# A two-layer diffusion backbone: the output projection of layer 1, three weight tiles split earlier, its first sums begun early, and x loaded into other places

## The chip, the cores and the metric

The kernel runs on one core of one Trainium2 chip. Five engines work side by side, each in its own fixed order: TensorE (PE: matmuls; PEld: loading of their stationary operand), VectorE (DVE), ScalarE (ACT), GpSimd (POOL) and SyncE (SP), which issues nearly all DMAs. They wait for each other by semaphores. The metric is the device time of one execution in microseconds (us).

## The reference, cut to what matters

Input: x (512 tokens of 1024), a context of 256 tokens, conditioning vectors, and float32 weights of two layers. Each layer is a mixer (attention) followed by a SwiGLU feed-forward network (FFN, hidden size 2816), both behind an RMS norm with adaptive scale and shift, both added to x through a gate. Layer 0 has windowed and dense attention; layer 1 has differential attention with 8 heads. Layer 1 is what the change touches:

```python
def finish(o):                                   # o: (b, n, 8 heads, 128)
    o = _rms(o, subln_w) * (1.0 - lam_init)      # norm over each head's 128
    return o.reshape(o.shape[0], o.shape[1], -1) @ w_out
o_x = _diff_attend(q_x, concat(k_c, k_x), concat(v_c, v_x), lam)
out_x = finish(o_x)                              # (512 x 1024) @ (1024 x 1024)
...
x = x + gx1 * ax                                 # the way out of the mixer
x = x + gx2 * _swiglu(_rms(x, norm_ffn_w[l]) * (1.0 + scx2) + shx2, ffn_w_in[l], ffn_w_out[l])
```

In the last layer only the 512 tokens of x go on; the context serves as keys and values.

## The kernel before, in words

**Tiles.** Tokens lie in tiles of 128: t = 0 to 3 are x, 4 and 5 the context. The model width 1024 is 8 K-tiles of 128. The operand of a projection lies transposed in hT (columns of x) and hTc (columns of the context), each as a pair: a rounded part "hi" and the rest "lo", both in float32r. A weight tile is split likewise: `unit` (L318) loads it into one of two raw buffers (tag "raw", L90), ACT rounds it (L326, woh), and DVE or POOL subtracts (L327, wol). Each product is then three matmuls, hi·hi, hi·lo, lo·hi (in the way out: L747, L748, L749). A tile of wor, woh and wol is one K-tile of the output weights, 512 KB raw.

**Layer 1's attention.** `in_proj1` (L593) makes q, k and v of one head for one token tile: projection (L422 to L424), copy qkv (L630), rotation, normalisation with rs_q on POOL (L156, L157), operands qd and kd, transposes (L651, L657). `attend1` (L664) has two parts: scores sc (L673, L674), maximum mx (DVE L676), exponentials e (ACT L678) and their combination (DVE L685); then transposes ppt (L692), the product with v, av (L700), and the norm of the head's result: o (ACT L702, L705), rs_o (POOL), o again (DVE L707). `Staggered` (L873) runs the second part of one tile behind the first part of the next. The stage's loop (L1063 on) goes over heads h and token tiles t, and `emit` (L1054) puts in the projections for a head about one head ahead: after h = 6, t = 0 the context tiles and tiles 0 and 1 of head 7 are in, after t = 2 all.

**The way out (OutProj, L718).** When all head projections are emitted (h = 7, t = 0), their pools are closed, and `out_units` (L710) loads and splits the 8 K-tiles of the output weights into the place that came free; every third raw tile goes to a place of its own, wor. `operand` (L725) loads the tile's x (`load_x`, L330), transposes its result o in two halves of 4 K-tiles (L737), and splits each half into hT (ACT L738, DVE L739). `sums` (L741) makes two halves of 512 columns, each 8 K-tiles of 3 matmuls in one PSUM bank; for tiles 0 to 2 both halves use the bank acc0, at low priority. `residual` (L426) multiplies by the gate (L429, into rtmp, one buffer) and adds to x (L430), on POOL for tiles 0 to 2 and on DVE for tile 3. Then `norm_steps` (L282) prepares FFN's operand: square (ACT L291), rs_n (POOL), scaling (ACT L293), transposes npt (PE L298), scale and shift (L304, L306), split (L308, L309). Its two work tiles, the room, are here the places of the context's hTc, two sets, used in turn.

**Places.** The tag "xo" has six places of 128 x 1024: layer 1's four results o_t lie in four of them, and x of tiles 0 and 1 can be loaded into the other two; x of tiles 2 and 3 takes the places of o of tiles 0 and 1 after their transposes. Split weights of the way out and of FFN share eight places each (tags whi and wlo).

**Order.** The order of each engine's instructions is fixed before the run: a planner goes by the order of the program, by priorities (`tc.high_priority`) and by its own estimate of the times.

Of the kernel before, what the change touches and what calls it, by code (L numbers as in the profile page):

```python
# [10 lines left out]
F32 = mybir.dt.float32  # L11
F32R = mybir.dt.float32r
# [51 lines left out]
def backbone(es: ExitStack, tc: tile.TileContext, x, c, ctx, c_ctx, mod_w, mod_b, norm_mix_w, norm_ffn_w,  # L64
# [48 lines left out]
    def f32(ap):  # L113
        return ap.bitcast(F32)
# [203 lines left out]
    def unit(pool, views, shape, bufs, name, sub=None, new_tile=raw_tile):  # L318

        raw = new_tile(shape, name + "r")  # L320
        for dst, src in views(raw):
            turn["load"] = nc.sync.dma_start(dst, src)
        p_hi, p_lo = pool if isinstance(pool, tuple) else (pool, pool)
        hi = p_hi.tile(shape, F32R, name=name + "h", tag="whi", bufs=bufs)
        lo = p_lo.tile(shape, F32R, name=name + "l", tag="wlo", bufs=bufs)
        nc.scalar.copy(hi, raw)  # L326
        (sub or nc.vector).tensor_sub(lo, raw, f32(hi))  # L327
        return hi, lo
# [378 lines left out]
        nc.vector.scalar_tensor_tensor(oc, oc, r, subln, ALU.mult, ALU.mult)  # L707


    def out_units(wp, w_out, subs=(nc.gpsimd,), rooms=(raw_tile,)):  # L710
        ws = []
        for k in range(KT):
            def views(raw, k=k):
                yield raw, w_out[0, k * P:(k + 1) * P, :]
            ws.append(unit(wp, views, [P, D], 8, "wo", subs[k % len(subs)], rooms[k % len(rooms)]))
        return ws

    class OutProj:  # L718

        def __init__(self, l, ws, o_t, xs, pool):  # L720
            self.l, self.ws, self.o_t, self.xs, self.g = l, ws, o_t, xs, {}
            for i in range(2 if l == 0 else 1):
                self.g[i] = gate_row(l, 2, i, pool)

        def operand(self, t):  # L725
            if self.xs[t] is None:
                self.xs[t] = load_x(t, self.l == 1)
            ohi, olo = tile_T(0, t), tile_T(1, t)
            if self.l == 0:
                nc.scalar.copy(ohi, self.o_t[t])  # L730
                nc.gpsimd.tensor_sub(olo, self.o_t[t], f32(ohi))
                return
            for q in range(2):
                pt = tr_tile("opt", [P, 4, P])
                for k in range(4):
                    kk = 4 * q + k
                    nc.tensor.transpose(pt[:, k, :], self.o_t[t][:, kk * P:(kk + 1) * P], ident)  # L737
                nc.scalar.copy(ohi[:, 4 * q:4 * q + 4], pt)  # L738
                nc.vector.tensor_sub(olo[:, 4 * q:4 * q + 4], pt, f32(ohi[:, 4 * q:4 * q + 4]))  # L739

        def sums(self, t, bank=None, pool=None, add=nc.vector):  # L741
            ohi, olo = tile_T(0, t), tile_T(1, t)
            for n in range(2):
                ps = acc_tile("ops", one=bank)
                for k in range(KT):
                    a, b = (z[:, n * 512:(n + 1) * 512] for z in self.ws[k])
                    nc.tensor.matmul(ps, ohi[:, k, :], a, start=k == 0, stop=False)  # L747
                    nc.tensor.matmul(ps, ohi[:, k, :], b, start=False, stop=False)  # L748
                    nc.tensor.matmul(ps, olo[:, k, :], a, start=False, stop=k == KT - 1)  # L749
# [194 lines left out]
    for b in range(4):  # L944
# [9 lines left out]
        if b == 3:  # L954
            att.flush()
            wp.close()
            even.close()
            wp = Pool("w0", "right")
            opa = Pool("opa")
            xs = [None] * NT  # L960
            oproj = OutProj(0, out_units(wp.pool, ev_w_out), o_t, xs, opa.pool)
        for t in order:
            for hp in range(2):
                if hp == 1:
# [191 lines left out]
```

## Time and profile before

| | us |
|---|---|
| median of 3 runs | 1808.97 (1807.68 to 1810.03) |
| profiled execution, its own time | 1809.96 |
| its span in the trace | 1808.2 |
| PE busy in the span | 1738.5 (96%) |
| layer 1's heads, first to last combination of exponentials (L685) | 1078.4 to 1362.1 |
| matmuls of layer 1's way out | 1354.5 to 1420.7 |

All times inside the execution count from the start of the span. A row of the order of time gives start, duration, engine, line, operation, output <- inputs, shapes and count; a bracket at its end tells how long the engine idled before it, and what released it. A busy PE is not PE at its peak: the granted clock (PEclk) says which share of full speed it had.

### The profile page before, as it was taken

The page shows a single profiled execution, that of the slowest core. Times are in us where ns is not written, and L with a number is a line of the kernel's source. Part 1 is how long each engine was busy: PE and PEld are TensorE (multiplying, and loading weights), DVE is VectorE, ACT ScalarE, POOL GpSimd, SP SyncE. Part 2 cuts the span into 40 slices and gives each one's busy share as a digit, 9 for nine tenths or more (in the row PEclk, how much of TensorE's full clock was granted, in tenths as well). Part 3 has the DMA queues.
Part 4 walks back from the last instruction along what each step waited for, and adds up shares of the span by engine and source line. Part 5 has one row for each costly group of instructions (what it writes and reads, how often), then busy time and mean ns, then how long its engine had stood idle before and what let it go on. Part 6 is the DMA issues. An engine that isn't in the chain of part 4 may idle for free. (4 is left out here: it accounts for less than half of the span.)

```text
span 1808.2 us, 26146 instructions
## 1 busy us (share of the span) xinstructions
PE 1738.5 (96%) x9958; PEld 1455.4 (80%) x9958; DVE 999.7 (55%) x1703; ACT 823.0 (46%) x1726; POOL 649.6 (36%) x840
## 2 busy tenths in 40 slices
PE   6999999999999999999999989999998999999998
PEld 4887776678888888888888889999986878888886
DVE  4765554444265555554543556766684455655653
ACT  6555555545354444343332656666573521231220
POOL 2774554632163344232220486667643200000000
PEclk8999999999999999999999999999999999999999
DMA  9112322303543234334320311111102333232331
GB/s 315 43 50 71 105 94 75 112 24 112 178 154 105 94 105 142 115 117 139 118 85 2 102 53 59 36 43 47 34 36 94 105 95 91 83 123 76 89 98 47
DMA packets 152477, 165.64 MB, mean 92 GB/s; under 512 B 16480, under 2 KB 139936, under 8 KB 152352
## 3 DMA queue, kind: packets, MB, share of 16 engines
q1 hardware_dynamic: 152000, 163.77, 28.9%
q8 instruction: 78, 1.28, 0.3%
q14 instruction: 47, 0.39, 0.1%
q10 hardware_dynamic: 352, 0.21, 0.0%
HBM read 159.73 MB, written 4.22 MB: 91 GB/s over the span
## 5 line engine op out<-in xcount | busy, mean ns | idle before, releaser
L785 PE MATMUL pg<-hT,wgh 128*128 128x512 f32 (+1 forms) x736 | 242.7, 384 | 0.0
L785 PE MATMUL pu<-hT,wuh 128*128 128x512 f32 (+1 forms) x736 | 242.2, 383 | 0.0
L429 DVE TENSOR_TENSOR dps<-dps,g 128x512 f32<-128x512 f32 x200 | 135.8, 697 | 142.4 <-PE dps L839 137.1
L837 PE MATMUL dps<-wdh,hdh 128*128 128x512 f32 x440 | 177.3, 404 | 8.7 <-ACT hdh L435 5.2
L838 PE MATMUL dps<-wdl,hdh 128*128 128x512 f32 x440 | 175.1, 398 | 0.0
L839 PE MATMUL dps<-wdh,hdl 128*128 128x512 f32 x440 | 166.4, 396 | 0.0
L785 PEld LDWEIGHTS pg<-hT,wgh 128*128 128x128 f32 x736 | 136.4, 188 | 30.9 <-issue 1.2
L785 PEld LDWEIGHTS pu<-hT,wuh 128*128 128x128 f32 x736 | 135.7, 188 | 28.7
L785 PE MATMUL pg<-hT,wgl 128*128 128x512 f32 (+1 forms) x368 | 141.4, 384 | 0.0
L785 PE MATMUL pu<-hT,wul 128*128 128x512 f32 (+1 forms) x368 | 140.9, 383 | 0.0
L430 DVE TENSOR_TENSOR x<-x,dps 128x512 f32<-128x512 f32 x200 | 133.2, 683 | 3.3
L422 PE MATMUL inps<-wih,hT 128*128 128x384 f32 x384 | 133.6, 348 | 0.9 <-ACT qkv L470 0.5
L424 PE MATMUL inps<-wih,hT 128*128 128x384 f32 x384 | 130.9, 342 | 0.0
L423 PE MATMUL inps<-wil,hT 128*128 128x384 f32 x384 | 130.7, 340 | 0.0
L206 ACT ACTIVATE modw<-modw,cols 128x256 f32<-128x256 f32 x192 | 82.0, 498 | 71.5 <-DMA modw<-in_mod_w_dram 64.5
L837 PEld LDWEIGHTS dps<-wdh,hdh 128*128 128x128 f32 x440 | 83.1, 189 | 31.7 <-ACT hdh L435 5.8
L327 DVE TENSOR_TENSOR wul<-wur,wuh 128x1024 fp32r<-128x1024 f32 x44 | 53.9, 1225 | 83.1 <-ACT wuh L326 83.1
L839 PEld LDWEIGHTS dps<-wdh,hdl 128*128 128x128 f32 x440 | 82.6, 188 | 19.9
L812 DVE TENSOR_TENSOR pu<-sg,pu 128x768 f32<-128x768 f32 (+1 forms) x44 | 36.4, 828 | 111.3 <-PE pu L785 96.9
L785 PE MATMUL pu<-hTc,wuh 128*128 128x256 f32 x352 | 97.9, 282 | 0.0
L838 PEld LDWEIGHTS dps<-wdl,hdh 128*128 128x128 f32 x440 | 83.3, 189 | 18.2 <-issue 0.4
L785 PE MATMUL pg<-hTc,wgh 128*128 128x256 f32 x352 | 97.8, 282 | 0.0
(235 smaller groups left out, 4289.4 us busy)
## 6 DMA issues: line engine op xcount, KB each, us to landing
modw<-in_mod_w_dram SPq DMA_DIRECT2D x96, 512.0 KB, 3.9
wgr<-in_ffn_w_in_dram SPq DMA_DIRECT2D x44, 512.0 KB, 3.5
wur<-in_ffn_w_in_dram SPq DMA_DIRECT2D x44, 512.0 KB, 3.6
wdr<-in_ffn_w_out_dram SPq DMA_DIRECT2D x44, 512.0 KB, 3.5
wir<-in_od_w_in_dram SPq DMA_DIRECT2D x96, 128.0 KB, 2.3
x<-in_x_dram SPq DMA_DIRECT2D x8, 512.0 KB, 3.8
wir<-in_ev_w_in_dram SPq DMA_DIRECT2D x16, 256.0 KB, 2.8
wor<-in_ev_w_out_dram SPq DMA_DIRECT2D x8, 512.0 KB, 3.4
```

The source lines that it names most:

```text
L206: nc.scalar.activation(pr[:, k], w[:, k], AF.Copy, scale=cols[:, kk:kk + 1])
L327: (sub or nc.vector).tensor_sub(lo, raw, f32(hi))
L422: nc.tensor.matmul(ps, hs[0][:, k, :], a, start=k == 0, stop=False)
L423: nc.tensor.matmul(ps, hs[0][:, k, :], b, start=False, stop=False)
L424: nc.tensor.matmul(ps, hs[1][:, k, :], a, start=False, stop=k == KT - 1)
L429: nc.vector.tensor_mul(tmp, ps, g[:, n * 512:(n + 1) * 512])
L430: eng.tensor_add(xt[:, n * 512:(n + 1) * 512], xt[:, n * 512:(n + 1) * 512], tmp)
L785: nc.tensor.matmul(ps[:, s0:s1], a, cols_T(b, s0, s1)[:, k, :], start=k == 0 and q == 0, stop=k == KT - 1 and q == 2)
L812: nc.vector.tensor_mul(pu, sg, pu)
L837: nc.tensor.matmul(ps, hh, a, start=j == 0, stop=False)
L838: nc.tensor.matmul(ps, hh, b, start=False, stop=False)
L839: nc.tensor.matmul(ps, hl, a, start=False, stop=j == nj - 1)
```

## The change

The change concerns where things lie, and when the planner may place them.

- After h = 6, t = 0, the first three K-tiles of the output weights are loaded and split, all three subtracted on POOL. Their places: for tile 0 the two free places of "xo"; for tiles 1 and 2 the two places of hTc. The other five are made where all eight were; they alternate between POOL (3, 5, 7) and DVE (4, 6) and use only the two raw buffers.
- After h = 6, t = 2, the first half (K-tiles 0 to 3) of tile 0's operand is transposed and split, and the matmuls of K-tiles 0 to 2 of its first 512 columns are issued into acc0. `sums` of tile 0 goes on from K-tile 3 (`begun`).
- In layer 1, x of each tile is loaded after the transposes of its o, and so into the places of o.
- The norm's room is one set of two tiles in the pool opa instead of two sets in hTc's places.
- The gates' loads are a method of their own; layer 0 does what it did.

```diff
-        p_hi, p_lo = pool if isinstance(pool, tuple) else (pool, pool)
+        p_hi, p_lo = pool if isinstance(pool, (list, tuple)) else (pool, pool)
...
+    class Place:
+        def __init__(self, ap):
+            self.ap = ap
+        def tile(self, *args, **kw):
+            return self.ap
...
-    def out_units(wp, w_out, subs=(nc.gpsimd,), rooms=(raw_tile,)):
+    def out_units(wp, w_out, subs=(nc.gpsimd,), ks=range(KT)):
         ws = []
-        for k in range(KT):
+        for k in ks:
             def views(raw, k=k):
                 yield raw, w_out[0, k * P:(k + 1) * P, :]
-            ws.append(unit(wp, views, [P, D], 8, "wo", subs[k % len(subs)], rooms[k % len(rooms)]))
+            ws.append(unit(wp[k] if isinstance(wp, list) else wp, views, [P, D], 8, "wo", subs[k % len(subs)]))
         return ws
...
-        def operand(self, t):
-            if self.xs[t] is None:
-                self.xs[t] = load_x(t, self.l == 1)
+        def operand(self, t, qs=range(2)):
+            if self.l == 0:
+                self.xs[t] = load_x(t)
...
-            for q in range(2):
+            for q in qs:
...
+            if 1 in qs:
+                self.xs[t] = load_x(t, True)
...
+        def half(self, ps, t, n, ks=range(KT)):
...
+        def sums(self, t, bank=None, pool=None, add=nc.vector, begun=None):
             for n in range(2):
-                ps = acc_tile("ops", one=bank)
...
+                ps = begun if begun is not None and n == 0 else acc_tile("ops", one=bank)
+                self.half(ps, t, n, range(3 if ps is begun else 0, KT))
                 residual(self.xs[t], ps, self.g[0 if t < NTX else 1], n, pool, add, 1)
...
-                ws = out_units(wp.pool, od_w_out, (nc.gpsimd, nc.vector), (raw_tile, raw_tile, lambda shape, name:
-                               opa.pool.tile(shape, F32, name=name, tag="wor", bufs=1)))
-                oproj = OutProj(1, ws, o_t, xs, opa.pool)
+                ws += out_units(wp.pool, od_w_out, (nc.vector, nc.gpsimd), range(3, KT))
+                oproj.gates(opa.pool)
             if h == 7 and 0 < t <= 3:
-                oproj.operand(t - 1)
+                oproj.operand(t - 1, range(t == 1, 2))
                 with tc.high_priority(-1000):
-                    oproj.sums(t - 1, 0, opa.pool, nc.gpsimd)
+                    oproj.sums(t - 1, 0, opa.pool, nc.gpsimd, begun if t == 1 else None)
             emit((h + 1) * NT + 2 + (2, 3, 5, 6)[t])
+            if h == 6 and t == 0:
+                free = [[keep.tile([P, D], F32R, name=name, tag="xo", bufs=6) for name in ("woh", "wol")]]
+                two = ctx_room([P, 2, D], F32R, "woc")
+                free += [[z[:, j] for z in two] for j in range(2)]
+                ws = out_units([[Place(z) for z in pair] for pair in free], od_w_out, ks=range(3))
+                oproj = OutProj(1, ws, o_t, xs)
+            if h == 6 and t == 2:
+                oproj.operand(0, (0,))
+                begun = acc_tile("ops", one=0)
+                oproj.half(begun, 0, 0, range(3))
     att.flush()
...
-    room = ctx_room([P, 2, KT, P], F32, "nroom")
+    room = [opa.pool.tile([P, KT, P], F32, name=name, tag=name) for name in ("nh", "nhc")]
     for t in range(NTX):
-        norm_hT(t, xs[t], 1, 1, None, room=[z[:, t % 2] for z in room])
+        norm_hT(t, xs[t], 1, 1, None, room=room)
```

More of the change, by code (lines that the diff above doesn't have):

```diff
@@ L739, in operand @@
                 nc.vector.tensor_sub(olo[:, 4 * q:4 * q + 4], pt, f32(ohi[:, 4 * q:4 * q + 4]))
-        def sums(self, t, bank=None, pool=None, add=nc.vector):
+            if 1 in qs:
+                self.xs[t] = load_x(t, True)
+        def half(self, ps, t, n, ks=range(KT)):
             ohi, olo = tile_T(0, t), tile_T(1, t)
-            for n in range(2):
-                ps = acc_tile("ops", one=bank)
[L745 to L749, printed above, removed]
+            for k in ks:
+                a, b = (z[:, n * 512:(n + 1) * 512] for z in self.ws[k])
+                nc.tensor.matmul(ps, ohi[:, k, :], a, start=k == 0, stop=False)
+                nc.tensor.matmul(ps, ohi[:, k, :], b, start=False, stop=False)
+                nc.tensor.matmul(ps, olo[:, k, :], a, start=False, stop=k == KT - 1)
+        def sums(self, t, bank=None, pool=None, add=nc.vector, begun=None):
+            for n in range(2):
+                ps = begun if begun is not None and n == 0 else acc_tile("ops", one=bank)
+                self.half(ps, t, n, range(3 if ps is begun else 0, KT))
                 residual(self.xs[t], ps, self.g[0 if t < NTX else 1], n, pool, add, 1)
@@ L960, in backbone @@
             xs = [None] * NT
-            oproj = OutProj(0, out_units(wp.pool, ev_w_out), o_t, xs, opa.pool)
+            oproj = OutProj(0, out_units(wp.pool, ev_w_out), o_t, xs)
+            oproj.gates(opa.pool)
         for t in order:
```

9 lines of the change are left out of this document (5 added, 4 removed).

## The prediction

> **What bounds the kernel now.** The page first: its engine shares and its chain say who sets the end.
>
> ```profile
> span 1808.2 us, 26146 instructions
> ...
> PE 1738.5 (96%) x9958; PEld 1455.4 (80%) x9958; DVE 999.7 (55%) x1703; ACT 823.0 (46%) x1726; POOL 649.6 (36%) x840
> ...
> PE 29%; DVE 4%; ACT 2%; issue 1%; POOL 0%; DMA 0%; POOLq 0%; ACTq 0%; DVEq 0%
> ```
>
> TensorE (PE) is busy for 96% of the span. Only time in which it idles, or runs at a lower clock, can be won. Next, therefore, busy time by stage (columns: stretch, its length, then busy us and instructions of PE, PEld, DVE, ACT, POOL, then granted clock, DMA share, GB/s). The change lies between 1294 and 1429 us.
>
> ```profile
> core 0: us, PE busy (x) PEld busy (x) DVE busy (x) ACT busy (x) POOL busy (x), PEclk, DMA share, GB/s
> 1200.00:1250.00 50.00, 49.37 (x342) 46.98 (x341) 35.59 (x67) 33.14 (x85) 33.66 (x52) 1.00 0.12 33
> ...
> 1305.00:1310.00 5.00, 5.00 (x28) 4.83 (x29) 1.09 (x4) 1.50 (x6) 2.83 (x7) 1.00 0.02 5
> 1310.00:1320.00 10.00, 9.72 (x67) 9.06 (x65) 7.39 (x15) 6.53 (x19) 4.11 (x8) 1.00 0.00 0
> 1320.00:1335.70 15.70, 15.64 (x111) 15.20 (x109) 12.98 (x27) 10.44 (x28) 7.46 (x14) 1.00 0.00 1
> 1335.70:1340.00 4.30, 2.03 (x11) 1.33 (x12) 2.26 (x5) 2.87 (x10) 2.35 (x5) 0.94 0.00 0
> 1340.00:1358.70 18.70, 17.31 (x103) 14.00 (x103) 17.04 (x24) 15.69 (x32) 7.29 (x7) 0.92 0.24 86
> 1358.70:1367.00 8.30, 2.95 (x20) 2.38 (x20) 6.60 (x9) 4.64 (x10) 4.14 (x4) 0.99 0.65 233
> 1367.00:1421.00 54.00, 52.61 (x257) 42.83 (x258) 20.31 (x34) 20.76 (x40) 15.59 (x20) 0.97 0.15 50
> ```
>
> Up to 1335.7 PE is full. Then it idles 2.27 us (4.30 - 2.03), 1.39, 5.35 and 1.39: 10.4 us, half of it in 1358.7 to 1367. The clock loses 8% of 17.31 us (1.4 us) from 1340 and 3% of 52.61 us (1.6 us) from 1367. About 13 us is the most that this place holds. What ends the large hole is read from PE's order of time, and from the chain there (start, us, what).
>
> ```profile
> 1304.23 0.28 PE L424 MATMUL inps<-wih,hTc 128*128 128x256 f32 x1
> ...
> 1352.86 1.50 PE L700 MATMUL av<-vv,PT 128*128 128x128 f32 x12
> ...
> 1361.83 0.50 PE L748 MATMUL ops<-wol,hT 128*128 128x512 f32 x1 [3.14 <-DVE wol L327]
> ...
> 1363.28 0.71 PE L737 MATMUL opt<-cst,o 128*128 128x128 f32 x5
> ...
> 1366.88 0.80 PE L747 MATMUL ops<-woh,hT 128*128 128x512 f32 x1 [0.94 <-ACT hT L738]
> ```
>
> ```profile
> 1359.35 2.42 DVE wol L327
> 1361.80 3.47 DMA wor<-in_od_w_out_dram
> 1365.29 1.05 ACT woh L326
> 1366.34 0.50 ACT hT L738
> 1366.88 0.80 PE ops L747
> ...
> 1375.61 0.23 PE ops L747
> ```
>
> The 3.14 us wait for the split of K-tile 3 stands first, but what follows it matters more: the first tile's K-tiles 4 to 7 begin at 1366.88, because their operand's cast (ACT, L738) stood behind the cast of weight tile 6, and that behind a DMA, and that behind a raw buffer which DVE freed late. The other waits for K-tile 7 of the operand, which needs head 7 of tile 0. Its way through the engines (ACT rows, then DVE, then POOL):
>
> ```profile
> 1354.16 2.94 ACT L326 CAST woh<-wor 128x1024 fp32r<-128x1024 f32 x3
> 1357.00 0.36 ACT L702 ACTIVATE o<-av,rc 128x128 f32<-128x128 f32 x1
> ...
> 1363.92 0.59 ACT L738 CAST hT<-opt 128x512 fp32r<-128x512 f32 x1 [1.68 <-PE opt L737]
> ```
>
> ```profile
> 1355.32 3.16 DVE L685 SCALAR_TENSOR_TENSOR e<-e,rt 128x768 f32<-128x768 f32 x1
> ...
> 1362.14 1.02 DVE L685 SCALAR_TENSOR_TENSOR e<-e,rt 128x768 f32<-128x768 f32 x1
> ...
> 1372.21 0.68 DVE L429 TENSOR_TENSOR rtmp<-ops,g 128x512 f32<-128x512 f32 x1
> ```
>
> ```profile
> 1355.27 5.42 POOL L327 TENSOR_TENSOR wol<-wor,woh 128x1024 fp32r<-128x1024 f32 x2 [1.77 <-ACT woh L326]
> ```
>
> The sums av of that head end at 1354.36 on PE; ACT takes them at 1357.00, after three weight casts. Two weight subtractions on POOL cover DVE's L685, which takes 3.16 us there and 1.02 alone.
>
> **The change, part by part.** The prices of one split (min/median/max in ns; first and last start), of the issue of a load of x (all four, from the view of its line) and of its landing (the two inside this stage, in us):
>
> ```profile
> L326 ACT CAST woh<-wor x8: 1034/1050/1056, 1340.3 to 1366.7; 128x1024 fp32r<-128x1024 f32 x8
> L327 POOL TENSOR_TENSOR wol<-wor,woh x4: 2366/2378/3067, 1341.4 to 1366.4; 128x1024 fp32r<-128x1024 f32 x4
> ...
> L327 DVE TENSOR_TENSOR wol<-wor,woh x4: 1220/2280/2514, 1342.3 to 1367.8; 128x1024 fp32r<-128x1024 f32 x4
> ```
>
> ```profile
> L333 SPq DMA_DIRECT2D x<-out_dram x4: 332/386/467, 1092.2 to 1379.9; - x4
> ```
>
> ```profile
> DMA to landing us min/median/max: 5.2/5.2/5.2
> ```
>
> **Three splits into head 6.** Three casts (3.15 us of ACT) and three subtractions, all on POOL (7.1 us), move ahead of 1335; of the five that stay, POOL has three and DVE two, where DVE had four of eight. SP's loads for tiles 0 to 4 are then done before 1340 (raw buffers come free one split at a time), those of 5 and 6 start when the pair 3 and 4 is split, and 7 follows alone: the row DMA, cast, operand cast of the chain is gone. The operand cast could follow its neighbour of 1363.92 at 1364.5 and end at 1365.1 instead of 1366.88: **-1.8** (ends 0, -1.8). With two tiles instead of three landing together, one cast of 1.05 us less stands ahead of L702: **-1.0** (ends 0 and -2.6, its whole delay). One POOL subtraction instead of two covers L685: half of 3.16 - 1.02 is **-1.0** (ends 0, -2.1). In head 6 the added work lies beside full PE: POOL was busy 14.4 of 30.7 us from 1305 to 1335.7, with 7.1 more 70%, which is the 33.66 of 50 us of an earlier head, where PE idled 0.63 us. At that rate 0.4 us in 30.7, of which 0.34 is there already; I take **+0.3** for jitter. The upper end: each subtraction costs DVE 2.14 us, 6.4 in all, against 2.72 us of slack in 1320 to 1335.7: +3.7. The places of tiles 1 and 2 are free after the last matmul on the context columns, 1304.5, and from 1305 to 1310 DVE has 1.09 us of work in 5.00, so I stay near the first.
>
> [...]
>
> **The first sums begun.** Nine matmuls (9 x 0.23 = 2.1 us) and four transposes (five took 0.71, so 0.6) leave the stage after 1340 for the 2.27 us of idle before it. Being filler in a stage whose hole is a wait, they win nothing by their own length; what they may win is the clock from 1340, at most 1.4, if PE does not idle before. Against it: in PE's order they stand before the last heads' scores, up to +2.7. I take half the clock, **-0.7**. The bank acc0 that they hold is asked by nobody till the tile's sums end. Their operand needs one cast (0.59) and one subtraction more ahead of 1340, on engines idle there for 1.4 and 2.0 us.
>
> [...]
>
> **The clock after 1367.** The hole gets shorter, but nine matmuls that lay in it are gone: half of 1.6, **-0.8** (ends 0, -1.6).
>
> **x in o's places.** Two loads of x that ran at 1092 and two at 1364 and 1380 become four, each issued on SP after its own tile's transposes, 0.39 us of issue and 5.2 to land. What is queued behind: behind the waiting load in SP stand the weight loads of the feed-forward network (FFN); behind the waiting addition on POOL stands the next tile's rs_o. For tiles 0 to 2 PE needs at least 12 matmuls with attention between (5.3 us from 1366.88 to the first product at 1372.2) or 24 (5.6 us): no wait. The last tile is tightest:
>
> ```profile
> 1409.50 0.27 PE L737 MATMUL opt<-cst,o 128*128 128x128 f32 x1
> ...
> 1415.63 0.69 DVE L430 TENSOR_TENSOR x<-x,ops 128x512 f32<-128x512 f32 x1
> ```
>
> Transposed at 1409.77, landed at 1415.4, needed at 1415.63: **0** (ends 0, +3.2 when one more load, 3.47 us by the chain, is ahead).
>
> **One room for the norm instead of two.** Tile 2's square must wait for tile 1's second transposes:
>
> ```profile
> 1424.92 1.07 ACT L291 ACTIVATE nroom<-x 128x1024 f32<-128x1024 f32 x1
> ...
> 1418.43 0.60 PE L298 MATMUL npt<-cst,nroom 128*128 128x128 f32 x4
> ...
> 1428.64 1.09 PE L298 MATMUL npt<-cst,nroom 128*128 128x128 f32 x8 [1.25 <-ACT nroom L293]
> ```
>
> So not before 1419.0. From a square to its transposes the last tile took 3.7 us (1424.92 to 1428.64), so tile 2's end near 1423.8 (1419.0 + 3.7 + 1.1), before the last tile's square at 1424.92. Behind the waiting square on ACT stand FFN's first weight casts; three of the eight slots for split weights are free now, so these can be done before: **0** (ends -1.25, the wait shown, and +3.7, one such chain, if the last square has to wait for all of tile 2).
>
> **The sum:** -1.8 - 1.0 - 1.0 + 0.3 - 0.7 - 0.8 = -5.0. The profiled execution took 1809.96 us in all (span 1808.2), 1.0 above the median of the runs. 1809.96 - 5.0 = 1804.96; on the scale of the medians, 1804.0.
>
> **The rivals.**
> **The last head holds the hole.** Weights are early, but head 7 of tile 0 becomes final no sooner (its five remaining splits in the way as before), and PE, with fewer matmuls left to fill, idles longer and runs colder. Only -1.8 and +0.3 stay: 1807.5. For it: PE's hole is mostly that operand. Against: three casts and POOL's 5.42 us stand visibly in its way.
> **PE stands in front of the begun sums** (the other sign). Nine matmuls and four transposes in PE's fixed order ahead of the scores wait for a split or for the operand as L748 did, 3.14 us, and then take 2.7: 5.8 us on attention's path, whose later gains vanish; with -1.8 and +0.3, +4.3: 1813.3. It is beyond 0.2% from a wait of 2.4 us. For it: the operand's cast and subtraction queue on ACT and DVE behind attention's. Against: tile 2 can be split long before, and its places are free early.
> **DVE held up in head 6** by the three POOL subtractions: +3.7 for +0.3, 1807.4. For it: POOL's order is fixed too, and a late place there can't be left. Against: the idle stretch after 1305. It decides from two of them after 1320 (4.3 us against 2.72).
> **x comes late:** one load of 3.47 us ahead of the last, +3.2: 1807.2. For it: SP's order is fixed, and FFN's loads are asked for in the same stretch. Against: they have no need to precede it.
>
> **How the numbers follow.** A difference below 0.2% (3.6 us) can't be told from none. Forecast 52%, the last head 20%, begun sums 14%, DVE 8%, x 6%. Forecast alone: 1798.2 (all good ends: -10.75) to 1805.4. Faster: the forecast and a bit of the last head, 54%; slower: the begun sums and a bad end of another, 16%; same 30%. The range, 1798.5 to 1812.5, takes in all cases but half of the begun sums' and the best ends.
>
> **What would show it.** Right: no wait of PE on wol, no wor load beside head 7's operand, three woh casts before 1335, L747 of K-tile 4 some 4 us earlier, clock near 1.00 from 1340. Wrong: PE waiting at K-tile 0 to 2 before 1340; a hole of over 6 us ended by ACT hT; POOL L430 ended by a DMA; npt of the last tile more than 8 us behind the last sums.

## The result, and the profile after

The changed kernel takes 1824.77 us in the median of six runs (1821.57 to 1825.36). The kernel before, run beside it, takes 1809.50 us (1805.10 to 1812.31). The ratio is 1.0086, with a 95% interval from 1.0075 to 1.0097: it is slower by some 15 us. The prediction said 1804.0 us, and its range ended at 1812.5. It was wrong, and on the wrong side.

The page of the profiled execution (1821.57 us, the shortest of the six) says little by its shares, which are nearly those of before: PE has as many matmuls, busy for 4.1 us longer.

```profile
PE 1742.6 (96%) x9958; PEld 1460.6 (80%) x9958; DVE 996.4 (55%) x1701; ACT 821.3 (45%) x1726; POOL 653.3 (36%) x842
```

The busy time by stage says more (columns as in the prediction; the stages lie some us later than before's).

```profile
core 0: us, PE busy (x) PEld busy (x) DVE busy (x) ACT busy (x) POOL busy (x), PEclk, DMA share, GB/s
...
1300.00:1310.00 10.00, 6.73 (x34) 6.59 (x35) 1.81 (x4) 3.98 (x10) 8.03 (x11) 0.83 0.38 117
...
1360.00:1370.00 10.00, 5.12 (x33) 3.86 (x33) 7.92 (x13) 8.54 (x20) 5.14 (x5) 0.96 0.40 125
1370.00:1380.00 10.00, 9.38 (x36) 7.35 (x37) 3.94 (x7) 1.87 (x6) 2.02 (x3) 0.69 0.38 144
...
1420.00:1430.00 10.00, 6.82 (x33) 5.50 (x32) 3.41 (x8) 5.15 (x11) 2.12 (x4) 0.87 0.00 0
1430.00:1440.00 10.00, 7.97 (x53) 7.78 (x52) 3.03 (x6) 5.18 (x10) 1.93 (x3) 0.79 0.00 0
```

Three places show PE idle at a lowered clock: 1300 to 1310, where before's 1305 to 1310 had PE full at 1.00; the known hole at 1360; and 1420 to 1440, behind the last output sums.

To compare executions that reach this place some us apart, I cut each at five events: the end of the last projection of a context tile (L424, hTc), the end of the last copy of a projection (L630), the start of the first tile's K-tile 4, behind its operand's second cast, the end of the last output sum, and the start of the last transposes npt of the norm. These rows of after's order of time give the cuts:

```profile
1300.65 0.28 PE L424 MATMUL inps<-wih,hTc 128*128 128x256 f32 x1
...
1333.74 0.48 ACT L630 COPY qkv<-inps 128x384 f32<-128x384 f32 x1 [0.85 <-PE inps L424]
...
1370.12 0.79 PE L758 MATMUL ops<-woh,hT 128*128 128x512 f32 x1 [1.96 <-ACT hT L748]
...
1423.87 0.40 PE L760 MATMUL ops<-woh,hT 128*128 128x512 f32 x1
...
1439.92 1.09 PE L298 MATMUL npt<-cst,nh 128*128 128x128 f32 x8 [2.03 <-ACT nh L293]
```

Of before, three of them stand in the prediction (1304.23, 1366.88, 1428.64), and these are the others:

```profile
1332.08 0.48 ACT L630 COPY qkv<-inps 128x384 f32<-128x384 f32 x1 [0.34 <-PE inps L424]
...
1420.50 0.40 PE L749 MATMUL ops<-woh,hT 128*128 128x512 f32 x1
```

| stage, us | before | after | difference |
|---|---|---|---|
| A: head 6, from the last context projection to the last copy | 28.05 | 33.29 | +5.2 |
| B: to the first tile's K-tile 4 | 34.32 | 35.90 | +1.6 |
| C: to the end of the output sums | 54.02 | 54.15 | +0.1 |
| D: to the last transposes of the norm | 7.74 | 15.65 | +7.9 |

Together +14.9 us, which is about the whole loss by the medians (15.3). The two profiled executions themselves lie only 11.5 us apart (spans of 1819.7 and 1808.2), because the changed one reaches the first cut 3.6 us earlier (1300.93 against 1304.51). That difference lies ahead of the stages, and executions differ there without any edit: in the kernel before with one room (first experiment), whose only edit lies behind the sums, the cut comes at 1301.61. One more caution: the cuts of A are ends on ACT and on one projection, and PE's order does not have the same matmuls on both sides of them in every kernel. The places are read one by one.

**Stage A.** The kernel before first, ACT and PE: the copy out of the bank, and the projection that follows without a wait.

```profile
1304.58 0.36 ACT L630 COPY qkv<-inps 128x256 f32<-128x256 f32 x1
```

```profile
1304.99 0.45 PE L422 MATMUL inps<-wih,hT 128*128 128x384 f32 x1
```

Then ACT, POOL and PE of the changed kernel, in order of time:

```profile
1301.90 0.30 ACT L641 CAST kd<-qy 128x128 fp32r<-128x128 f32 x1 [5.02 <-POOL qy L633]
...
1302.36 1.98 ACT L326 CAST woc<-wor 128x1024 fp32r<-128x1024 f32 x2
1304.24 0.37 ACT L630 COPY qkv<-inps 128x256 f32<-128x256 f32 x1
```

```profile
1296.45 2.40 POOL L327 TENSOR_TENSOR wol<-wor,woh 128x1024 fp32r<-128x1024 f32 x1
...
1300.41 0.19 POOL L156 TENSOR_SCALAR rs_q<-qss 128x2 f32<-128x2 f32 x1 [0.67 <-DVE qss L378]
...
1301.47 0.40 POOL L633 TENSOR_TENSOR qy<-qy,rs_q 128x128 f32<-128x128 f32 x1
```

```profile
1301.07 0.33 PE L657 MATMUL kpt<-identr,kd 128*128 128x128 f32 x2
1304.67 0.69 PE L422 MATMUL inps<-wih,hT 128*128 128x384 f32 x1 [3.27 <-ACT qkv L630]
1305.15 0.53 PE L423 MATMUL inps<-wil,hT 128*128 128x384 f32 x1
...
1307.39 0.53 PE L424 MATMUL inps<-wih,hT 128*128 128x384 f32 x1
...
1307.96 0.34 PE L423 MATMUL inps<-wil,hT 128*128 128x384 f32 x1
```

The next projection needs the PSUM bank that the copy L630 empties. Two things stand in front of that copy in fixed orders: on ACT the two casts of K-tiles 1 and 2 (1.98 us), and further back on POOL the subtraction of K-tile 0 (2.40 us), behind which kd, rs_q and qy wait. The last 0.67 us before rs_q are a wait for DVE's qss: DVE's order has it behind L707, which ran beside that subtraction and took 2.48 us, where its median is 0.35 (last section). So DVE has a part in the hole, of 0.67 us by this row. PE idles 3.27 us, and then its matmuls follow each other at 0.32 us (seven steps from 1305.15 to 1307.39) until 1307.71, in place of 0.17: the granted clock is 0.50 from 1304.67 to 1307.71, where before's was 1.00 (1305 to 1310).

That adds up. In stage A PE idles 3.55 us in place of 0.29 (+3.3), nine slow matmuls cost 9 x 0.146 = 1.3, and PE's order has two matmuls more ahead of the last copy (183 in place of 181, some 0.5 us).

**Stage B.** ACT around the last head's operand:

```profile
1359.24 1.04 ACT L326 CAST woh<-wor 128x1024 fp32r<-128x1024 f32 x1 [2.03 <-DMA wor<-in_od_w_out_dram]
1360.19 0.36 ACT L702 ACTIVATE o<-av,rc 128x128 f32<-128x128 f32 x1
1360.50 1.05 ACT L326 CAST wgh<-wgr 128x1024 fp32r<-128x1024 f32 x1
...
1364.24 0.59 ACT L748 CAST hT<-opt 128x512 fp32r<-128x512 f32 x1
...
1366.20 1.05 ACT L326 CAST wgh<-wgr 128x1024 fp32r<-128x1024 f32 x1 [1.07 <-DMA wgr<-in_ffn_w_in_dram]
...
1368.53 1.05 ACT L326 CAST wuh<-wur 128x1024 fp32r<-128x1024 f32 x1 [0.39 <-DMA wur<-in_ffn_w_in_dram]
1369.49 0.58 ACT L748 CAST hT<-opt 128x512 fp32r<-128x512 f32 x1
```

And PE, which needs the bank that L702 empties:

```profile
1360.60 1.60 PE L700 MATMUL av<-vv,PT 128*128 128x128 f32 x12 [1.73 <-ACT o L702]
```

The cast of K-tile 7 waits 2.03 us for its load, and stands in front of the scaling L702 of head 6's last tile, for which PE waits in turn; head 7's first tile is scaled only at 1363.99. Before, three casts without a wait stood in front of head 7's scaling, and the cast that waited for its load in front of the operand's. Three casts of FFN's first weights have been added: the early K-tiles leave three of the eight weight slots free, and the planner fills them in the middle of the hole. That these cost the 1.6 us is a theory at this point.

**Stage D.** The norm with one room, first ACT's squares (L291), then PE:

```profile
1416.46 1.06 ACT L291 ACTIVATE nh<-x 128x1024 f32<-128x1024 f32 x1 [3.16 <-PE npt L298]
...
1425.23 1.06 ACT L291 ACTIVATE nh<-x 128x1024 f32<-128x1024 f32 x1 [4.68 <-issue]
...
1434.82 1.06 ACT L291 ACTIVATE nh<-x 128x1024 f32<-128x1024 f32 x1 [4.99 <-issue]
```

```profile
1424.11 1.04 PE L298 MATMUL npt<-cst,nh 128*128 128x128 f32 x8
1428.33 0.58 PE L802 MATMUL pg<-hT,wgh 128*128 128x256 f32 x1 [3.18 <-ACT hT L308]
1433.28 1.46 PE L298 MATMUL npt<-cst,nh 128*128 128x128 f32 x8
1439.92 1.09 PE L298 MATMUL npt<-cst,nh 128*128 128x128 f32 x8 [2.03 <-ACT nh L293]
```

Each square now begins right after the transposes of the tile before it (1424.11 + 1.04, then 1425.23; 1433.28 + 1.46, then 1434.82). For these two the view names no releaser ("issue"), and the reading goes by the times; for the first it names npt. Those stand in PE's order behind whatever PE has to do, once behind a wait of its own (3.18 us). Tiles 1, 2 and 3 follow each other at 9.2 and 6.6 us (1424.11, 1433.28, 1439.92), all behind the last sum. Before, tile 2's square ran while PE was still at the sums:

```profile
1413.95 1.07 ACT L291 ACTIVATE nroom<-x 128x1024 f32<-128x1024 f32 x1
```

### The profile page after: what moved, and what is told of

Same layout as the page of the kernel before. It is cut to its first block, busy times and chain, and to the rows that moved or that the text cites. A ratio compares the mean times of both kernels' runs of the same rounds, so it can differ in the third digit from the quotient of the medians.

```text
span 1819.7 us, 26152 instructions
## 1 busy us (share of the span) xinstructions
PE 1742.6 (96%) x9958; PEld 1460.6 (80%) x9958; DVE 996.4 (55%) x1701; ACT 821.3 (45%) x1726; POOL 653.3 (36%) x842
## 5 line engine op out<-in xcount | busy, mean ns | idle before, releaser
L430 DVE TENSOR_TENSOR x<-x,dps 128x512 f32<-128x512 f32 x200 | 133.1, 683 | 3.3
L424 PE MATMUL inps<-wih,hT 128*128 128x384 f32 x384 | 131.5, 343 | 0.0
```

What stands on the lines that cost most here:

```text
L424: nc.tensor.matmul(ps, hs[1][:, k, :], a, start=False, stop=k == KT - 1)
L430: eng.tensor_add(xt[:, n * 512:(n + 1) * 512], xt[:, n * 512:(n + 1) * 512], tmp)
```

## The experiments

My theory after these traces: A, B and D are separate losses of 5.2, 1.6 and 7.9 us; each has its own cause in the order of the instructions, and each can be undone alone. Rivals stand with each run. All ratios are to the kernel before, run beside them, and are not the quotients of the two medians; a tenth of a per cent is 1.8 us. b_one_room, a_behind, a_hold_sq0 and a2_rooms were compared with 12 runs of it (1808.52 us), a_behind12, a_w_behind and a_all_nobegun with 21 others (1808.99 us).

**D alone: the kernel before with one room.**

```diff
-    room = ctx_room([P, 2, KT, P], F32, "nroom")
+    room = [z[:, 0] for z in ctx_room([P, 1, KT, P], F32, "nroom")]
...
-        norm_hT(t, xs[t], 1, 1, None, room=[z[:, t % 2] for z in room])
+        norm_hT(t, xs[t], 1, 1, None, room=room)
```

> The kernel before, with one room for the norm of the four tiles instead of two; nothing else of the change. Theory (of the 15 us lost, about 8 are lost behind the last output sums, because each tile's square waits for the transposes of the tile before it, and those come late in PE's order): about 1817 us, some 8 above the kernel before, with the last transposes of the norm 13 to 16 us behind the last sums instead of 8. Rival (the room costs nothing by itself, as the prediction had it, and the late end of the norm comes from what stands before it): within 2 us of the kernel before, 1808 to 1812.

1814.48 us, ratio 1.0035 (1.002 to 1.005), so 6.3 us (3.6 to 9.0). A, B and C are 28.05, 34.38 and 52.92 us, D is 14.80 in place of 7.74. The rival of 2 us falls. The single room costs its 6 to 7 us by itself; the 8 us that I expected were somewhat too many.

**A alone: the early splits behind the copy.** The mark is the copy L630 of context tile 5. The planner may place the splits only after it.

```diff
-            nc.scalar.copy(raw[:, :n], ps)
+            turn[f"qkv{t}"] = nc.scalar.copy(raw[:, :n], ps)
...
-                ws = out_units([[Place(z) for z in pair] for pair in free], od_w_out, ks=range(3))
+                with behind("qkv5"):
+                    ws = out_units([[Place(z) for z in pair] for pair in free], od_w_out, ks=range(3))
```

> The changed kernel; the splits of the three early K-tiles are issued behind the copy of the second context tile's projection out of its bank, so that their casts stand after that copy in ACT's order. Theory (5 us are lost in head 6 because the early cast stands in front of the copy that frees the bank for the next projection, and the clock falls in the 3.3 us hole): about 1820 us, 4 to 5 below the changed kernel, no wait of PE of over 1 us near the last context projection, and a granted clock of 1.00 there. Rival (head 6 is long because the three subtractions on POOL hold DVE up, wherever they stand): 1823 to 1826, head 6 as long as in the changed kernel.

1817.78 us, ratio 1.0054 (1.0039 to 1.007), 5.8 us less than the changed kernel's 1.0086. Its stage in windows and ACT in order of time:

```profile
1300.00:1310.00 10.00, 9.98 (x65) 9.58 (x64) 4.19 (x8) 6.87 (x15) 7.83 (x10) 1.00 0.35 102
```

```profile
1301.02 0.36 ACT L630 COPY qkv<-inps 128x256 f32<-128x256 f32 x1
1301.27 1.06 ACT L326 CAST woh<-wor 128x1024 fp32r<-128x1024 f32 x1
```

The same casts a little later (that of K-tile 2 follows at 1302.23), and PE has no hole (9.98 of 10 us) at a full clock. Stage A is 27.09 us: 6.2 below the changed kernel, and 1.0 below the kernel before. (That 1.0 is no gain of its own: PE idles 0.02 us in place of 0.29, and 176 matmuls in place of 181 stand ahead of the last copy.) So three subtractions on POOL in head 6 cost nothing where they stand now. The rival (DVE held up wherever they stand) falls.

**Which of the two in front of the copy?** Only K-tiles 1 and 2 are moved; K-tile 0 stays.

```diff
+                rooms = [[Place(z) for z in pair] for pair in free]
+                ws = out_units(rooms, od_w_out, ks=range(1))
+                with behind("qkv5"):
+                    ws += out_units(rooms, od_w_out, ks=range(1, 3))
```

> The changed kernel; only K-tiles 1 and 2 (into the context columns) are split behind the second context tile's copy, K-tile 0 stays where the change put it. It parts the two things that stood ahead of that copy: K-tile 0's subtraction on POOL (2.4 us, in front of the scaling of q and k) and the two casts of K-tiles 1 and 2 on ACT (2.0 us, right in front of the copy). Theory (both count, and the colder clock comes only with the whole hole): 1819.5 to 1822 us, head 6 about 30 us in place of 33.3 and of the 27.1 with all three moved. Rival (the casts alone did it): 1817 to 1819, head 6 27 to 28. Second rival (K-tile 0's subtraction alone did it): 1823 or more, head 6 over 32.

1817.03 us (five runs), 1.0055 (1.0043 to 1.0068), as with all three moved; stage A is 28.65 us. PE in order of time:

```profile
1306.36 0.33 PE L657 MATMUL kpt<-identr,kd 128*128 128x128 f32 x2
1308.08 0.44 PE L422 MATMUL inps<-wih,hT 128*128 128x384 f32 x1 [1.38 <-ACT qkv L630]
1308.36 0.33 PE L423 MATMUL inps<-wil,hT 128*128 128x384 f32 x1
1308.53 0.34 PE L424 MATMUL inps<-wih,hT 128*128 128x384 f32 x1
```

The two casts made 4.6 of the 6.2 us in this stage (some 1 us of it only by four matmuls that now stand on the other side of the cut), K-tile 0's subtraction the other 1.6 (its hole of 1.38 us is still there). In the time of the whole, K-tile 0's part cannot be seen. My expectation that both count alike was off; the first rival is nearest. Behind the hole of 1.38 us the matmuls follow at 0.17 us at once, and the granted clock from 1306 to 1310 is 1.00, in place of the 0.50 behind the hole of 3.27 us.

**B alone: FFN's first weights behind the norm's first square.**

```diff
-        turn["square"] = nc.scalar.activation(h, xt, AF.Square, accum_out=ss)
+        turn[f"square{t}"] = turn["square"] = nc.scalar.activation(h, xt, AF.Square, accum_out=ss)
...
-                    with behind(*(("square",) if p == 0 and name == "wu" and u else ())):
+                    with behind(*(("square",) if p == 0 and name == "wu" and u else ("square0",) if p == 0 and l == 1 else ())):
```

> The changed kernel; the first gate and up weights of the feed-forward network are split only behind the first norm's square, and no longer in the hole of the last head. Theory (the hole is 1.6 us longer because these casts and subtractions stand in front of the last head's operand): 1821 to 1823 us, 2 to 4 below the changed kernel, with K-tile 4 of the first tile 2 to 4 us earlier against the last projection. Rival (the hole is set by the last head's own way through DVE and ACT, and the early weights help the feed-forward network to start): 1824 to 1828, no gain or a loss.

1821.95 us, 1.0074 (1.0056 to 1.0092). Against the changed kernel's 1.0086 that is 2 us, which these intervals can't tell from nothing. The trace says more: stage B is 33.31 us in place of 35.90, with A and D unchanged (33.25, 15.63). But FFN's casts are not all that sets this stage: in a_behind12, with two of them in the hole as well, B is 31.94 us. There K-tile 7's cast waits only 0.17 us for its load. What of the 1.6 us is due to which cast stays open.

**D in the changed kernel.** First with two K-tiles early instead of three, so that one pair of context places holds a second room:

```diff
-                two = ctx_room([P, 2, D], F32R, "woc")
-                free += [[z[:, j] for z in two] for j in range(2)]
-                ws = out_units([[Place(z) for z in pair] for pair in free], od_w_out, ks=range(3))
+                two = keep.tile([P, 2, D], F32R, name="woc", tag="hTc0")
+                free.append([two[:, j] for j in range(2)])
+                ws = out_units([[Place(z) for z in pair] for pair in free], od_w_out, ks=range(2))
...
-    room = [opa.pool.tile([P, KT, P], F32, name=name, tag=name) for name in ("nh", "nhc")]
+    rooms = [[opa.pool.tile([P, KT, P], F32, name=name, tag=name) for name in ("nh", "nhc")]]
+    other = keep.tile([P, 2, KT, P], F32, name="nroom", tag="hTc1")
+    rooms.append([other[:, j] for j in range(2)])
```

> The changed kernel with two K-tiles split early instead of three (the second in the context columns of the high parts), so that the context columns of the low parts hold a second room for the norm. Theory: the norm's 8 us come back, and one split less in head 6 may give another 0 to 2: 1815 to 1818 us, the norm's last transposes about 8 us behind the last sums. Rival (the norm is late for another reason, or the sixth split in the last head takes the gain): 1822 to 1826.

(The ranges of the begun sums and of the later splits go by two as well, and the norm takes `rooms[t % 2]`.) 1816.16 us, 1.0044 (1.0027 to 1.006): 7.6 us less than changed; D is 6.08 us, A 31.92 and C 56.84 (+2.7). Then with three K-tiles early, as the change has it, and the second room in one of the free weight slots (n = 1; this run, a_nobegun, a_w_behind_hold and a_w3_behind were compared with 27 runs of the kernel before, 1808.15 us):

```diff
+    rooms = [[opa.pool.tile([P, KT, P], F32, name=name, tag=name) for name in ("nh", "nhc")]]
+    rooms += [[wp.pool.tile([P, KT, P], F32R, name=f"n{tag}{j}", tag=tag, bufs=8).bitcast(F32) for tag in ("whi", "wlo")] for j in range(n)]
...
-        norm_hT(t, xs[t], 1, 1, None, room=room)
+        norm_hT(t, xs[t], 1, 1, None, room=rooms[t % (n + 1)])
```

> The changed kernel with three K-tiles early as it is, and a second room for the norm in one of the three slots of split weights that they leave free. Theory (the single room costs 7 to 8 us): 1814 to 1817.5 us, the norm's last transposes 6 to 9 us behind the last sums in place of 15.7, head 6 as long as in the changed kernel (33.3 us from the last context projection to the last copy of a projection). Rival (with two rooms and three early tiles the feed-forward network lacks the slot, and starts as late): 1821 or more.

1815.46 us, 1.0037 (1.0025 to 1.0049), 8.9 us less than changed; D is 7.04 us, A still 33.38. It does a little more than its name: the room's use of a slot moves the planner's FFN casts out of the hole too, and B is 32.48 us.

**Begun sums undone.**

```diff
-            if h == 6 and t == 2:
-                oproj.operand(0, (0,))
-                begun = acc_tile("ops", one=0)
-                oproj.half(begun, 0, 0, range(3))
```

(and `operand` and `sums` of tile 0 called whole.)

> The changed kernel without its begun sums: three K-tiles early, all sums of the first tile after the last head's start. The prediction gave the begun sums 0.7 us of gain (ends 1.4 of gain, 2.7 of loss). Theory (they ran at 1345 to 1349, in time that PE had, and shorten what is left to do in the last head): 1824.5 to 1827 us, 0 to 2 above the changed kernel. Rival (they and the four transposes stand in PE's order ahead of the last heads' scores, and cost more than they save): 1821 to 1823.5.

1822.18 us, 1.0078 (1.0063 to 1.0093): not to be told from the changed kernel. In the trace, K-tile 4 comes 1.3 us later (B 37.23) and the sums behind it take 2.5 us less (C 51.63). The second number is no effect of the edit that this trace can show: in the 13.1 us behind K-tile 4 the granted clock was 1.00, in the changed kernel's trace 0.77, and that clock differs between executions of one order too (the repaired kernel, below).

**The repairs together.** The splits behind the copy, the second room in a weight slot, and FFN's splits behind the first square:

> All three repairs on the changed kernel: early splits behind the second context tile's copy, a second room for the norm in a free weight slot, the feed-forward network's first splits behind the norm's first square. Theory, from the stages of the runs so far (27.1 us for head 6, 86.7 to the end of the sums, 7.7 to the norm's last transposes; the kernel before has 28.1, 88.3 and 7.7): 121.5 in place of 124.1 us, so 1805 to 1808, the first version below the kernel before. Rival (the repairs overlap, since PE fills its idle time from one pool of work): 1809 to 1813.

1806.95 us, 0.9996 (0.9982 to 1.001). The third edit turned out to be idle: with the room in a slot the order of the instructions is the same without it. So the next kernel is this one measured again, in a later group of runs (kernel before: 21 runs, 1808.99 us):

> The two repairs that matter in the instructions' order: early splits behind the copy, a second norm room in a free weight slot (which by itself keeps the feed-forward network's first splits out of the hole). The order of the instructions is that of the kernel with all three repairs, so the theory expects the same time, 1804 to 1810 us; it is here beside the version without begun sums, on the same chip. Rival: none; a difference of over 2 us would be scatter.

1806.48 us, 0.9987 (0.9977 to 0.9997). Two measurements of one order: 0.7 and 2.4 us below the kernel before, under the 0.2% that can be told. Their traces show how far one stage can scatter: K-tile 4 follows the same waits (1.56 us for DVE's hT, then 0.68 and 0.67 us for ACT's), but in the 13.4 us from there the granted clock is 1.00 in one and 0.78 in the other, and C is 54.29 and 56.38 us. From the changed kernel it is 16 to 18 us; the single repairs add to 14.7 (5.8 and 8.9). A is 27.1 us in both, B 33.04 and 32.91. So the theory holds in its sum for A and D, and the repaired change is worth about nothing.

Three rooms in all three free slots, with the splits behind the copy (the edit above with n = 3):

> The changed kernel with the early splits behind the second context tile's copy, and three more rooms for the norm, in all three free weight slots: each of the four tiles has its own, and the feed-forward network's weights find no slot before the norm is through with one. Theory: the stages as with all three repairs, 1804 to 1809 us; more than two rooms bring nothing more, since PE's order sets the transposes. Rival (the feed-forward network's first weights come so late now that its first sums wait for them): 1812 or more, with PE idle behind the norm.

1813.25 us, 1.0031 (1.0018 to 1.0044); here the rival was right. Windows and PE's order behind the sums:

```profile
1420.00:1440.00 20.00, 17.04 (x117) 16.34 (x118) 8.80 (x11) 8.70 (x12) 2.15 (x2) 0.76 0.46 146
```

```profile
1420.02 0.80 PE L802 MATMUL pg<-hT,wgh 128*128 128x256 f32 x2 [4.60 <-ACT wgh L326]
```

FFN's weights now find no slot in time. PE waits 4.60 us for the first of them and runs at 0.76. With one slot given to the norm FFN had two left, and its first matmuls waited 0.5 us at most; with all three given away they wait for weights.

The repaired kernel without begun sums (with a_w_behind, in the same group of runs):

> The repaired kernel (early splits behind the copy, a second norm room in a free weight slot, no early splits for the feed-forward network in the hole) without the begun sums. In the changed kernel leaving them out changed nothing that could be told. Theory (they are filler for PE, and where they stand makes little difference): within 3 us of the repaired kernel, 1804 to 1810. Rival (once the other losses are repaired, the begun sums' place between the last heads' scores costs what the prediction's upper end had, 2.7 us or more): below 1804, the first version clearly faster than the kernel before. Second rival (they shorten the last head's stage): 1810 or more.

1808.07 us, 0.9998 (0.9989 to 1.0007): the theory, no difference that can be told. By stage, against the trace of the same order with begun sums and the same clock behind K-tile 4 (a_w_behind_hold, 1.00 in both), B is 35.85 in place of 33.04 us and C 54.19 in place of 54.29. In this one pair of traces the begun sums shorten B by 2.8 us, and the times of the whole do not show it.

**Where is the gain that the prediction saw?** In the repaired kernel K-tile 4 comes 1.3 and 1.4 us earlier than before, not 3.8 and more. Two last runs ask why (kernel before: 23 runs, 1808.82 us). In the first, the cast of K-tile 7 stands behind the scaling L702 of head 7's first tile:

```diff
-                ws += out_units(wp.pool, od_w_out, (nc.vector, nc.gpsimd), range(3, KT))
+                ws += out_units(wp.pool, od_w_out, (nc.vector, nc.gpsimd), range(3, KT - 1))
...
+                if t == 1:
+                    with behind("o70"):
+                        ws += out_units(wp.pool, od_w_out, (nc.vector, nc.gpsimd), range(KT - 1, KT))
```

> The repaired kernel (early splits behind the copy, second norm room in a free weight slot); the cast of K-tile 7, which still waits 1.9 us for its load in front of the scaling of head 6's and head 7's outputs on ACT, stands behind that scaling now. Theory (this wait is what is left of the chain that the prediction thought gone): K-tile 4 of the first tile begins 1 to 2 us earlier, 1803 to 1806 us. Rival (the last head's own rows of scores, exponentials and sums set the hole): within 1 us of the repaired kernel, 1806 to 1808.5, with PE waiting for the operand all the same.

1808.27 us, 0.9995 (0.9984 to 1.0006). ACT and PE of this kernel:

```profile
1356.38 0.36 ACT L702 ACTIVATE o<-av,rc 128x128 f32<-128x128 f32 x1
1356.63 1.04 ACT L326 CAST woh<-wor 128x1024 fp32r<-128x1024 f32 x1
```

```profile
1362.39 0.66 PE L692 MATMUL ppt<-cst,e 128*128 128x128 f32 x4 [2.58 <-DVE hT L749]
1363.87 0.79 PE L758 MATMUL ops<-woh,hT 128*128 128x512 f32 x1 [0.68 <-ACT hT L748]
```

No cast in front of that scaling waits for a load over 0.21 us any more, and B is 32.89 us all the same. PE waits for a split instead (2.58 us): the subtraction L749 of tile 1's first half, which stands on DVE behind the last heads' combination of exponentials (L685, 1.02 us from 1360.72) and ends at 1362.33. K-tile 7 of the first tile is transposed on PE right behind that wait. The rival holds. In the second, K-tile 5 gets a raw buffer of its own:

```diff
-                ws += out_units(wp.pool, od_w_out, (nc.vector, nc.gpsimd), range(3, KT))
+                ws += out_units(wp.pool, od_w_out, (nc.vector, nc.gpsimd), range(3, KT),
+                                lambda shape, name: opa.pool.tile(shape, F32, name=name, tag="nh"))
```

(`out_units` uses this place for K-tile 5 alone.)

> The repaired kernel with a raw buffer of its own for K-tile 5 (in the norm's room, which is not in use by then), so that K-tiles 3 to 5 are loaded at once and 6 and 7 follow two by two. The casts of K-tiles 5 to 7 then stand together in front of the scaling of head 7's output. Theory (a cast that waits for a load is the loss, not the cast): no wait of ACT for a load of over 0.5 us there, 1804 to 1807 us. Rival (three casts of 1.05 us in a row in front of that scaling cost as much as one that waits 1.9 us): 1807 to 1810.

1809.45 us, 1.0002 (0.999 to 1.0013). No load is waited for, and three casts of 2.92 us stand in a row in front of L702: B is 35.06 us, worse by 2.1. My theory, that the wait is the loss and the casts are not, falls in both runs.

## Why the prediction was wrong, point by point

- **Head 6, +0.3 (upper end +3.7): +5.2 measured.** This is the first step that failed. The prediction weighed busy shares (POOL at 70%) and DVE's slack. It never asked which instruction stands behind the casts in ACT's order. The answer was the copy that empties the bank of the next projection. The term was 3.3 us of hole and a lost clock (1.3). The +3.7 that the prediction named for its upper end was the time by which DVE would run out of slack; DVE's stretch did come (L707 2.48 us), but its part in the hole was 0.67 us, through rs_q. The same splits a few instructions later cost nothing (stage A 27.1).
- **One room, 0 (ends -1.25 and +3.7): +7.9 measured, 6.3 alone.** The prediction saw that tile 2's square waits for tile 1's transposes, and then counted one chain of 3.7 us. The chain is 9.2 and 6.6 us: on PE the transposes wait behind other work, and on ACT the square and scaling stand among L304 and L308 of the tile before. Nor does it start at 1419.0, as assumed, but at 1424.11, where PE's order put tile 1's transposes, behind the last sum. Its upper end allowed one late square; all of tiles 1 to 3 came late.
- **FFN's first casts "can be done before":** counted as a benefit of three free slots. They were done before, in the hole; held back, B is 2.6 us shorter (33.31), though a_behind12 shows that the same casts can stand there at less cost (31.94).
- **The hole, -1.8 and -1.0:** failed. The load that a cast waits for was not gone; it became that of K-tile 7 (2.03 us). But this was not the cause either. With no such wait (a_last2), B is 1.4 us below before, with the casts together (a_raw3) 0.7 above. The prediction's rival "the last head holds the hole" fits the repaired kernels best. It priced the time at 1807.5 us, and they took 1806.5 and 1807.0; but no gain at all would lie as near, so the agreement of the number is partly luck, and that PE runs colder there is shown by one of their two traces only (0.78; 1.00 in the other).
- **One subtraction less over L685, -1.0:** the stretch went wholly, not by half (the last five L685 take 1.01 to 1.02 us, where one took 3.16 before), and the time shows no gain from it beyond the 1.4 us.
- **Begun sums, -0.7 and the rival of +5.8:** the sums ran at 1345.32 to 1349.1, after the idle time they were meant for, and PE waited for no K-tile of 0 to 2. Neither gain nor loss can be told in the time, of the changed kernel or of the repaired one; one pair of traces has 2.8 us of gain in B. The rival with the other sign, which I had named as the danger, did not happen.
- **The clock after 1367, -0.8:** an estimate, and not shown. In the 13.1 us from K-tile 4 before had 0.87 and the changed kernel 0.77. But one order with the same waits gave 1.00 and 0.78 in two traces, 2.1 us of stage C: the length of the hole alone does not decide this term. The hole of 5.35 us that it goes by was three waits, too (3.14, 1.29 and 0.94 us in before's order of time), with matmuls between them.
- **x in o's places, 0: right.** The view of rtmp's instructions on POOL, the six additions L430, names one releaser (idle us in all, times):

```profile
  DVE rtmp L429: 31.1, 6
```

All six waited for the product, none for a load. The last tile, which the prediction called the tightest, is added on DVE, and its first addition (1419.47) begins right behind its product (1418.74 + 0.70).

Of the signs the prediction named, two came true: the hole ended by ACT's hT (6.1 us of idle between 1358.87 and 1370.12, in several waits), and the last transposes 15.7 us behind the last sums. PE at K-tiles 0 to 2 and L430 behind a DMA did not.

Of the 4.6 us of stage A between a_behind12 and the changed kernel, PE's idle time makes 2.2 (3.55 less 1.38), the slow matmuls 1.3, and four matmuls of scores more ahead of the last copy most of the rest: that part is work on the other side of the cut, no loss. What stays open: how stage B's difference divides among the casts in it, why the clock behind K-tile 4 differs from one execution to the next, and x in o's places, which was not run alone.

## What to carry to other kernels

An engine with idle time is not a free place: before moving work onto it, read its order at that spot, and ask which bank or buffer the next instruction in line sets free. A buffer given up is priced by the whole loop that it closes (square, scaling, transposes, and all that stands between them in each engine's order), not by one link. And a place that comes free will be used by the next in line: look who that is, and whether it can then stand in front of the critical operand.

## What the runs showed of the hardware

Behind the hole of 3.27 us PE's granted clock was 0.50 for the next 3.0 us (1304.67 to 1307.71; 0.32 us from matmul to matmul until then, 0.17 after it). Behind the one of 1.38 us at the same place (a_behind12) it was 1.00. The three other kernels that kept the hole (a_hold_sq0, a_nobegun and a_w; 3.27, 3.26 and 3.26 us) show the same 0.32 us behind it, so none of the four traces has the full clock there. In a2_rooms, where the hole is 2.33 us, the 0.32 us begins at the fourth matmul behind it (1308.30) and lasts until 1311.18. Shorter waits in a row ahead of K-tile 4 were not followed by the same clock in two executions of one order: behind 1.56 and 0.68 us it was 1.00 in one trace (a_w_behind_hold), and behind 1.56 and 0.67 us 0.78 in the other (a_w_behind), over the next 13.4 us. What decides it, these traces do not show.

While POOL subtracted K-tile 0 (2.40 us from 1296.45), DVE's small L707, which takes 0.35 us in the median of its 32 times, took seven times as long:

```profile
1296.51 2.48 DVE L707 SCALAR_TENSOR_TENSOR o<-o,rs_o,subln 128x128 f32<-128x128 f32 x1 [0.72 <-POOL rs_o L157]
```

It ended within 0.14 us of POOL's instruction (1298.99 and 1298.85); what held it up, the rows do not name. The prediction's +3.7 us for it did not show in the time: where the splits stood behind the copy, PE idled 0.02 us in stage A.
